# Two-layer trunk on one core: the triangular inverse on VectorE, and plain block products for the first two items of each seven-product projection

## The chip, the core and the metric

The program runs on one core of a Trainium2 chip. A core has TensorE (PE in the profile: matrix products, with its weight loads shown apart as PEld), VectorE (DVE), ScalarE (ACT), GpSimd (POOL) and SyncE (SP, which here only starts DMAs). TensorE writes to PSUM; the working memory is SBUF. The metric is the device time of one execution in microseconds: 3083.43 us is the median of three runs (3078.94 to 3089.16). The profile shows one more execution, which took 3091.84 us; its span from the first to the last instruction is 3090.0 us.

## The reference

A sequence of 1024 positions of width 1024 goes through two layers. Each layer is a mixer and a feed-forward part (FFN), both with a modulation by a condition vector and a layer norm at the end:

```
for i in range(DEPTH):
    mod = (e @ ada_w[i] + ada_b[i])[:, None, :]
    sh1, sc1, g1, sh2, sc2, g2 = jnp.split(mod, 6, axis=-1)
    y = mixers[i % N_MIXERS](x * (1.0 + sc1) + sh1)
    x = layer_norm(DN_ALPHA * x + (1.0 + g1) * y, ln_g[i, 0], ln_b[i, 0])
    y = conv_ffn(x * (1.0 + sc2) + sh2, ffn_up[i], ffn_conv_w[i], ffn_conv_b[i], ffn_down[i])
    x = layer_norm(DN_ALPHA * x + (1.0 + g2) * y, ln_g[i, 1], ln_b[i, 1])
```

The mixer of layer 0 is a gated delta net with 8 heads. It needs, for each head and each block of 64 positions, the solution of a triangular system:

```
kk = jnp.where(strict, jnp.einsum('bhncd,bhnmd->bhncm', kb, k) * decay, 0.0)
sol = lax.linalg.triangular_solve(kk + eye, rhs, left_side=True, lower=True, unit_diagonal=True)
```

and then a scan over the blocks with a state. The mixer of layer 1 is a retention with 4 heads: a projection to q, k, v and a gate of 2048 columns, a scan, and an output projection. The FFN projects 1024 to 2 x 2816 columns (gate and up), convolves the gate over three positions, and projects back.

## The kernel before

**Numbers.** Every large product is done in float32r with two halves of each operand: a value is split into a rounded high part (ScalarE copy, L89) and a low part (value minus high part, L90 on VectorE or GpSimd), and a product is three matmuls (L110 to L112). A weight block of 128 x 1024 is split whole by `load_w` (tiles wr, wh, wl); one of 128 x 512 is split by `block` (tile wb).

**Stages in order.** Gated delta net (up to about 660 us of the span), its output projection and layer norm, FFN of layer 0 (a projection up from about 775 us, a projection down), retention (its projection from about 1484 us, scan, output projection), FFN of layer 1 (projection up from about 2381 us, projection down).

**The gated delta net.** Heads go in four pairs. For a pair, `t_path` builds the blocks X, transposes them on VectorE into Y (L738), inverts the 32 x 32 triangular blocks by forward substitution (31 steps, each a product L746 into the tile fs and a subtraction L748 into T, both on GpSimd), and transposes T on VectorE into RX (L751) and a copy of it, by ScalarE, into TX (L755). `t_chain` (tile R), `prep` (L857, VectorE), `dt_half` (L892, VectorE) and `scan` use the result. `filler` gives TensorE other work meanwhile: projections of the other heads, whose convolution is three VectorE instructions per half (L450, `conv_half`), and z projections without one. The order of TensorE's instructions is written out by a planner, `run`: it keeps a clock, picks among the streams by priority, and takes the length of a wait from the table LAT; a step of the forward substitution counts LAT["fs"] = 1.03 us. On the other engines a scheduler sets the order at build time.

**The seven-product projection.** `strassen` multiplies the activations (cut in 2 x 2 blocks of four tiles each: B11, B12, B21, B22) with a list of items, each two units of 128 columns of weights. It is called three times: FFN up of layer 0, the q, k and gate projection of retention, FFN up of layer 1. An item in the steady state (`wino`, n of 2 or more) does seven block products of 12 matmuls; operand sums of the weights are formed by `psub` on VectorE in PSUM (L1131). The operand sums of the activations, T1 to T4, are formed by `build_T`: it transposes the normalized rows (L405, TensorE), scales them (L407, ScalarE), and forms T3 = B22 - B12, T2 = T3 + B11, T1 = B22 - T2 and T4 = B21 - T2, each split into halves.

B11 and B21 come from the first half of the sequence and are ready early; B12 and B22 come from the second half, whose layer norm ends just before. So the first two items are handled apart. `early` does, for each of them, the products of B11 and B21 with two blocks of the first unit (48 matmuls for both items) while the layer norm ends. Then the generators `wino(0)` and `wino(1)` form the sums of the weights on GpSimd (L1143 to L1146, tile ws), do the other five products, in two parts with the sums of `rest` between them, and add up the results on VectorE. In `build_T` the table BAL gives GpSimd the splits of T1 and T4 and one of B22 ("b1": 15, "b4": 15, "b2": 8), and the two sums of T4 are on GpSimd as well (L429, L430). GpSimd also computes a power for the layer norm (L339, L1313), which the normalization on VectorE or ScalarE (L284, L282) waits for.

Of the kernel before, what the change touches and what calls it, by code (L numbers as in the profile page):

```python
# [28 lines left out]
BAL = {"r11": 0, "r12": 0, "r22": 0, "rS1": 0, "rS2": 0, "rS3": 0, "rS4": 0, "rw21": 0, "rwT1": 0, "rwT2": 0, "rwT3": 0, "rwT4": 0, "rn": 0, "rh": 1, "011": 0, "012": 0, "022": 0, "0S1": 0, "0S2": 0, "0S3": 0, "0S4": 0, "0w21": 0, "0wT1": 0, "0wT2": 0, "0wT3": 0, "0wT4": 0, "0n": 1, "0h": 0, "f11": 0, "f12": 0, "f22": 0, "fS1": 0, "fS2": 0, "fS3": 0, "fS4": 0, "fw21": 0, "fwT1": 0, "fwT2": 0, "fwT3": 0, "fwT4": 0, "fn": 1, "fh": 0, "gw": 0, "gh": 0, "gn": 3, "b1": 15, "b2": 8, "b3": 0, "b4": 15, "bT": 0, "ba": 0, "rw11": 0, "rw22": 0, "0w11": 0, "0w22": 0, "fw11": 0, "fw22": 0}  # L29
# [4 lines left out]
def trunk_kernel(ctx: ExitStack, tc, A):  # L34
# [357 lines left out]
    def build_T(B, xts, scale, shift, tags):  # L392
        for nm in ("T1", "T2", "T3", "T4", "22"):
            B[nm] = [None] * 4
        tags = dict(zip(("T1", "T2", "T3", "T4", "22"), tags))
# [15 lines left out]
        for k, tg in enumerate((("qkv", "qkv"), ("qkv", "qkv"), ("t2", "t2"), ("t2", "ada"))):  # L411
            b12, b22 = load(k, tg[0]), load(4 + k, tg[1])
            put("22", k, b22, pool if BAL["b2"] & 1 << k else dve)
            dve.tensor_sub(b12, b22, b12)
            put("T3", k, b12, pool if BAL["b3"] & 1 << k else dve)
            raw.append((b12, b22))

        def rest():
            for k in range(4):
                t3, b22 = raw[k]  # L420
                h11, l11 = B["11"][k]
                h21, l21 = B["21"][k]
                e1 = pool if BAL["ba"] & 1 << k else dve
                e1.tensor_tensor(t3, t3, h11, ALU.add)
# [5 lines left out]
                pool.tensor_tensor(t3, t3, l21, ALU.add)  # L430
                put("T4", k, t3, pool if BAL["b4"] & 1 << k else dve)
# [1439 lines left out]
```

## Time and profile before

| | |
|---|---|
| median of three runs | 3083.43 us |
| profiled execution | 3091.84 us, span 3090.0 us |
| PE busy in the span | 2830.1 us (92%), 13434 matmuls |
| DVE busy | 2306.9 us (75%), 3705 instructions |
| ACT busy | 1316.8 us (43%) |
| POOL busy | 968.8 us (31%), 966 instructions |
| mean granted TensorE clock | 0.966 |

Busy time of PE is the sum over pipelined matmuls, so a stage with 90% can be without any gap. A timeline row gives start, length, engine, line, operation, output and input tiles, and, in brackets, the idle time in front of it with the instruction that ended it. A windows row gives, for each engine, busy time and number of instructions in a stretch, then the granted TensorE clock as a share of full speed, the DMA share and the GB/s. A waits row gives the total, the number and the longest of the waits of one kind.

### The profile page before, as it was taken

The page shows a single profiled execution, that of the slowest core. Times are in us where ns is not written, and L with a number is a line of the kernel's source. Part 1 is how long each engine was busy: PE and PEld are TensorE (multiplying, and loading weights), DVE is VectorE, ACT ScalarE, POOL GpSimd, SP SyncE. Part 2 cuts the span into 40 slices and gives each one's busy share as a digit, 9 for nine tenths or more (in the row PEclk, how much of TensorE's full clock was granted, in tenths as well). Part 3 has the DMA queues.
Part 4 walks back from the last instruction along what each step waited for, and adds up shares of the span by engine and source line. Part 5 has one row for each costly group of instructions (what it writes and reads, how often), then busy time and mean ns, then how long its engine had stood idle before and what let it go on. Part 6 is the DMA issues. An engine that isn't in the chain of part 4 may idle for free.

```text
span 3090.0 us, 38786 instructions
## 1 busy us (share of the span) xinstructions
PE 2830.1 (92%) x13434; PEld 2286.9 (74%) x13434; DVE 2306.9 (75%) x3705; ACT 1316.8 (43%) x2412; POOL 968.8 (31%) x966
## 2 busy tenths in 40 slices
PE   6979989999799999998799999999998899999996
PEld 5867767777678878786677787767776678887785
DVE  6766767465888888987777745566688987777988
ACT  3744655433444444445332342221343544444442
POOL 0366274333511111730422302522201511113604
PEclk9999999999899999999899999999999999999998
DMA  7231222243254444854233444655654242335653
GB/s 271 76 105 63 79 75 77 82 157 136 84 171 157 157 153 157 320 175 145 102 110 109 160 159 135 205 173 179 194 206 145 95 147 103 103 103 206 235 179 119
DMA packets 242596, 448.65 MB, mean 145 GB/s; under 512 B 22880, under 2 KB 76384, under 8 KB 242400
## 3 DMA queue, kind: packets, MB, share of 16 engines
q1 hardware_dynamic: 211216, 398.45, 39.0%
q10 hardware_dynamic: 29760, 43.00, 3.8%
q0 software_dynamic: 1424, 4.72, 0.4%
q8 instruction: 106, 1.74, 0.2%
q14 instruction: 90, 0.74, 0.1%
HBM read 337.55 MB, written 108.53 MB: 144 GB/s over the span
## 4 chain that ended last, share of the span: by engine, by line
PE 31%; DVE 9%; DMA 5%; issue 4%; POOL 2%; ACT 1%; SPq 0%; POOLq 0%; DVEq 0%; ACTq 0%
PE acc L580 5%; PE acc L1092 5%; PE sc L1092 2%; PE acc L110 2%; PE acc L112 2%; PE acc L111 2%; PE sc L580 2%; PE acc L275 2%; PE acc L276 2%; PE acc L277 1%; DMA wr<-in_ret_wqk 1%; PE sc L111 1%; PE sc L112 1%; PE sc L110 1%; DVE wb L90 1%
## 5 line engine op out<-in xcount | busy, mean ns | idle before, releaser
L1505 POOL TENSOR_TENSOR o<-o 128x512 f32<-128x512 f32 x88 | 117.4, 1344 | 627.2 <-DVE o L1498 618.6
L580 PE MATMUL acc<-hT,wh 128*128 128x512 f32 x960 | 300.4, 394 | 0.0
L275 PE MATMUL acc<-bb,ab 128*128 128x512 f32 x504 | 193.0, 409 | 32.6 <-DVE ab L90 18.7
L1092 PE MATMUL acc<-T,wb 128*128 128x512 f32 x840 | 207.7, 397 | 14.5 <-DVE wb L90 14.5
L276 PE MATMUL acc<-bb,ab 128*128 128x512 f32 x504 | 205.1, 407 | 9.9 <-DVE bb L90 9.8
L580 PEld LDWEIGHTS acc<-hT,wh 128*128 128x128 f32 x960 | 182.8, 190 | 33.9
L580 PE MATMUL acc<-hT,wl 128*128 128x512 f32 x480 | 203.7, 424 | 3.2 <-ACT sq L469 2.1
L90 DVE TENSOR_TENSOR ab<-ar,ab 128x512 fp32r<-128x512 f32 x210 | 181.5, 872 | 30.7 <-ACT ab L89 30.4
L89 ACT ACTIVATE ab<-ar 128x512 fp32r<-128x512 f32 x210 | 128.6, 623 | 174.8 <-PE acc L277 86.6
L277 PE MATMUL acc<-bb,ab 128*128 128x512 f32 x504 | 202.8, 404 | 0.0
L1092 PEld LDWEIGHTS acc<-T,wb 128*128 128x128 f32 x840 | 159.4, 191 | 52.7 <-DVE wb L90 19.4
L90 DVE TENSOR_TENSOR wb<-wr,wb 128x512 fp32r<-128x512 f32 x168 | 121.2, 724 | 97.8 <-ACT wb L89 96.7
L90 DVE TENSOR_TENSOR wb<-mm,wb 128x512 fp32r<-128x512 f32 x216 | 144.9, 683 | 21.0 <-ACT wb L89 19.0
L1171 ACT ACTIVATE pc<-acc 128x512 f32<-128x512 f32 x140 | 83.0, 593 | 170.1 <-PE acc L1092 99.4
L89 ACT ACTIVATE wb<-mm 128x512 fp32r<-128x512 f32 x216 | 122.5, 593 | 69.9 <-DVE mm L1131 68.1
L89 ACT ACTIVATE wb<-wr 128x512 fp32r<-128x512 f32 x168 | 102.8, 626 | 110.9 <-DMA wr<-in_ffn_up 48.0
L450 DVE SCALAR_TENSOR_TENSOR qkv<-raw,vc,qkv 128x512 f32<-128x512 f32 x144 | 125.9, 878 | 29.7 <-ACT qkv L448 26.2
L110 PE MATMUL acc<-T,wb 128*128 128x512 f32 x340 | 136.4, 403 | 11.4 <-DVE wb L90 6.4
L275 PEld LDWEIGHTS acc<-bb,ab 128*128 128x128 f32 x504 | 97.5, 195 | 61.3 <-DVE ab L90 14.3
L90 DVE TENSOR_TENSOR wl<-wr,wh 128x1024 fp32r<-128x1024 f32 x67 | 91.1, 1360 | 64.5 <-ACT wh L89 64.0
L1484 DVE SCALAR_TENSOR_TENSOR o<-g,vc,o 128x512 f32<-128x512 f32 (+2 forms) x176 | 136.5, 793 | 2.5 <-ACT o L1479 1.8
L580 PE MATMUL acc<-wh,hT 128*128 128x512 f32 x384 | 137.1, 419 | 1.2 <-DVE vv L90 1.2
(556 smaller groups left out, 8035.3 us busy)
## 6 DMA issues: line engine op xcount, KB each, us to landing
wr<-in_ffn_up SPq DMA_DIRECT2D x94, 512.0 KB, 4.1
mvw<-in_ada_w SPq DMA_DIRECT2D x80, 512.0 KB, 4.3
ad<-o SPq DMA_DIRECT2D x154, 256.0 KB, 2.1
ar<-ad SPq DMA_DIRECT2D x154, 256.0 KB, 3.8
Br<-in_ffn_down SPq DMA_DIRECT2D x88, 256.0 KB, 3.4
wr<-in_ret_wv SPq DMA_DIRECT2D x32, 512.0 KB, 3.7
ar<-od SPq DMA_DIRECT2D x56, 256.0 KB, 5.1
xs<-xt ACTq DMA_DIRECT2D x24, 512.0 KB, 4.9
```

The lines of the kernel that those rows point to most:

```text
L89: act.activation(dst_h, src, AF.Copy)
L90: eng.tensor_tensor(dst_l, src, dst_h, ALU.subtract)
L110: mm(acc, wl[:, k], hl[0], start=first, stop=False)
L111: mm(acc, wh[:, k], hl[1], start=False, stop=False)
L275: mm(acc, a[1][:, sl], w[0], start=first, stop=False)
L276: mm(acc, a[0][:, sl], w[1], start=False, stop=False)
L277: mm(acc, a[0][:, sl], w[0], start=False, stop=last)
L450: dve.scalar_tensor_tensor(oh, raw[:, 3 - j:515 - j], w[:, 3 - j:4 - j], oh, ALU.mult, ALU.add)
L580: pq(pe.matmul(out, lhsT, rhs, start=start, stop=stop), cost)
L1092: return pe.matmul(*a, skip_group_check=True, **kw)
L1484: dve.scalar_tensor_tensor(tv, gv[:, c0 - j:c1 - j], w[:, 2 - j:3 - j], tv, ALU.mult, ALU.add)
L1505: pool.tensor_tensor(o[d], o[x], o[y], op)
```

## The change

Four things change.

1. The forward substitution of the triangular inverse (L746, L748) is issued on VectorE instead of GpSimd, and LAT["fs"] goes from 1.03 to 1.3, so that the planner writes another order for TensorE in the gated delta net.
2. The first two items of each `strassen` call are computed with plain block products: eight products of 12 matmuls instead of seven, 192 matmuls for both items instead of 168. `early` is replaced by `side`. Side 0 (B11 with B21, both units of both items, 96 matmuls) comes before the transposes, side 1 (B12 with B22, 96 matmuls) after them. No sums of weights are needed, so L1143 to L1146 and the additions of the results are gone. Weights are loaded and split whole, by `load_w`, eight times per call.
3. In `build_T` B12 itself is now split and kept as well (in the buffers of T1); the sums are formed from it in another order, one more than before for each of the four tiles of T1, and all sums and all splits are on VectorE (b1, b2, b3, b4 are 0). `rest` is issued after side 1 of the first item.
4. In the retention call (`direct`) the results of side 0 go straight from PSUM through the gate's activation to memory; in the FFN calls ScalarE copies them to SBUF first.

```diff
-BAL = {... "b1": 15, "b2": 8, "b3": 0, "b4": 15, "bT": 0, "ba": 0, ...}
+BAL = {... "b1": 0, "b2": 0, "b3": 0, "b4": 0, "bT": 0, "ba": 0, ...}
...
             b12, b22 = load(k, tg[0]), load(4 + k, tg[1])
+            put("12", k, b12, pool if BAL["b3"] & 1 << k else dve)
             put("22", k, b22, pool if BAL["b2"] & 1 << k else dve)
-            dve.tensor_sub(b12, b22, b12)
-            put("T3", k, b12, pool if BAL["b3"] & 1 << k else dve)
             raw.append((b12, b22))

         def rest():
             for k in range(4):
-                t3, b22 = raw[k]
+                t1, b22 = raw[k]
                 h11, l11 = B["11"][k]
                 h21, l21 = B["21"][k]
+                dve.tensor_sub(b22, b22, t1)
+                put("T3", k, b22, pool if BAL["b3"] & 1 << k else dve)
                 e1 = pool if BAL["ba"] & 1 << k else dve
-                e1.tensor_tensor(t3, t3, h11, ALU.add)
-                e1.tensor_tensor(t3, t3, l11, ALU.add)
-                dve.tensor_sub(b22, b22, t3)
-                put("T1", k, b22, pool if BAL["b1"] & 1 << k else dve)
-                put("T2", k, t3, pool if BAL["bT"] & 1 << k else dve)
-                pool.tensor_tensor(t3, h21, t3, ALU.subtract)
-                pool.tensor_tensor(t3, t3, l21, ALU.add)
-                put("T4", k, t3, pool if BAL["b4"] & 1 << k else dve)
+                e1.tensor_tensor(b22, b22, h11, ALU.add)
+                e1.tensor_tensor(b22, b22, l11, ALU.add)
+                put("T2", k, b22, pool if BAL["bT"] & 1 << k else dve)
+                dve.tensor_sub(t1, t1, h11)
+                dve.tensor_sub(t1, t1, l11)
+                put("T1", k, t1, pool if BAL["b1"] & 1 << k else dve)
+                e4 = pool if BAL["b4"] & 1 << k else dve
+                e4.tensor_tensor(b22, h21, b22, ALU.subtract)
+                e4.tensor_tensor(b22, b22, l21, ALU.add)
+                put("T4", k, b22, e4)
...
-            pool.tensor_tensor(tv, bc(Y[:, j + 1:, j], nj), bm(T[:, j, 0:nj], ni), ALU.mult)
+            dve.tensor_tensor(tv, bc(Y[:, j + 1:, j], nj), bm(T[:, j, 0:nj], ni), ALU.mult)
             ts_ = T[:, j + 1:, 0:nj]
-            pool.tensor_tensor(ts_, ts_, tv, ALU.subtract)
+            dve.tensor_tensor(ts_, ts_, tv, ALU.subtract)
             yield LAT["fs"]
...
-        def early(u):
-            w = load_w(u)
+        def side(n, s):
             out = []
-            for b in ("11", "21"):
+            for u in items[n][:2]:
+                w = load_w(u)
                 X = acc_tile()
-                for k in range(4):
-                    mm3(X, w, k + (4 if out else 0), B[b][k], k == 0, k == 3)
-                out.append(tl("cv", [P, 516], name="p1")[:, 0:HALF])
...
+                for i, b in enumerate((("11", "21"), ("12", "22"))[s]):
+                    for k in range(4):
+                        mm3(X, w, k + 4 * i, B[b][k], i == 0 and k == 0, i == 1 and k == 3)
+                out.append(X)
             return out
...
-        ws = [wino(n, items[n][2]()) for n in range(2)]
-        for w in ws:
-            next(w)
-        rest()
...
+        for n in range(2):
+            if not direct:
+                sinks.append(items[n][2]())
+                for i in range(2):
+                    sinks[n](2 * i, ahead[n][i], None)
+            X = side(n, 1)
+            for i in range(2):
+                sinks[n](2 * i + 1, X[i], None)
+            if n == 0:
+                rest()
+            if items[n][3]:
+                items[n][3]()
+        for n in range(2, len(items)):
+            wino(n, items[n][2]())
+            if items[n][3]:
+                items[n][3]()
```

The order in which the engines get their instructions moves at three places that matter below. In the rows, the words in brackets are the semaphores that an instruction waits on, named by engine or DMA queue; line numbers of the changed kernel are 1 to 4 higher in its first half and up to 11 lower in its last part.

**VectorE at the end of the forward substitution of the first pair.** Before, VectorE runs convolutions of the filler (L450, tile qkv) and a weight split (wl), and then takes the transpose RX as soon as GpSimd has finished T:

```order
L90 TENSOR_TENSOR wl<-wr,wh 128x1024 [waits DMAHW3_49,PE_49,Activation_49]
L450 SCALAR_TENSOR_TENSOR qkv<-raw,vc,qkv 128x512 [waits DVE_49]
L450 SCALAR_TENSOR_TENSOR qkv<-raw,vc,qkv 128x512 [waits Activation_49,Pool_49]
L450 SCALAR_TENSOR_TENSOR qkv<-raw,vc,qkv 128x512 [waits DVE_49] x2
L751 STREAM_TRANSPOSE RX<-T 128x1024 [waits Pool_49]
L755 STREAM_TRANSPOSE TX<-TP 128x1024 [waits Activation_49]
L857 TENSOR_TENSOR qkv<-mm,ir 128x512 [waits PE_49]
```

In the changed kernel, at the start of the same substitution, its steps (L750 and L752) stand among the convolutions (L454):

```order
L742 STREAM_TRANSPOSE Y<-X 128x1024 [waits Activation_49]
L454 SCALAR_TENSOR_TENSOR qkv<-raw,vc,qkv 128x512 [waits DVE_49]
L750 TENSOR_TENSOR fs<-Y,T 128x31 [waits DVE_49,Pool_49]
L752 TENSOR_TENSOR T<-T,fs 128x31 [waits DVE_49]
L750 TENSOR_TENSOR fs<-Y,T 128x60 [waits DVE_49]
L454 SCALAR_TENSOR_TENSOR qkv<-raw,vc,qkv 128x512 [waits Activation_49]
L752 TENSOR_TENSOR T<-T,fs 128x30x2 [waits DVE_49]
L454 SCALAR_TENSOR_TENSOR qkv<-raw,vc,qkv 128x512 [waits DVE_49]
L750 TENSOR_TENSOR fs<-Y,T 128x87 [waits DVE_49]
```

The 62 instructions of a pair moved from GpSimd's queue into VectorE's, each behind the one before it by a wait, and other work stands between them.

**GpSimd at the layer norm in front of the retention projection.** Before, the powers for the norm (L1313, tile mv) stand behind the sums of the weights (tile ws), which wait for the DMA of the weights:

```order
L1313 TENSOR_TENSOR mv<-mv,mhalf 128x1 [waits DVE_49]
L1146 TENSOR_TENSOR ws<-wr,ws 128x512 [waits Pool_49]
L1313 TENSOR_TENSOR mv<-mv,mhalf 128x1 [waits DVE_49]
L1143 TENSOR_TENSOR ws<-wr 128x512 [waits DMAHW0_49]
L1144 TENSOR_TENSOR ws<-ws,wr 128x512 [waits DMAHW7_49,Pool_49]
L1145 TENSOR_TENSOR ws<-wr 128x512
L1313 TENSOR_TENSOR mv<-mv,mhalf 128x1 [waits DVE_49,Activation_49]
```

Now they (L1302) follow the norm's gain (L1287) directly, and the next thing on GpSimd belongs to the third item (tile rm):

```order
L1287 TENSOR_TENSOR xt<-xt,rowb 128x512 [waits DMAHW6_49,DMASW7_49]
L1287 TENSOR_TENSOR xt<-xt,rowb 128x512
L1287 TENSOR_TENSOR xt<-xt,rowb 128x512 [waits Pool_49] x3
L1302 TENSOR_TENSOR mv<-mv,mhalf 128x1 [waits DVE_49] x6
L1302 TENSOR_TENSOR mv<-mv,mhalf 128x1 [waits DVE_49,Activation_49] x2
L1529 DMA dx<-in_dx 128x1024 [waits DMAHW6_49,DMAHW4_49,PE_49]
L1561 TENSOR_TENSOR rm<-pc,sinT 128x512 [waits DMAHW2_49,DMAHW7_49,DVE_49,PE_49]
```

The sums of the weights have left the queue in front of the powers.

**The sums of the activations in the first projection.** Before, GpSimd forms T4 (L429, L430, tile bt) and splits T1, T4 and one of B22, while VectorE does the rest:

```order
L90 TENSOR_TENSOR T_7238<-bt,T_7238 128x512 [waits Activation_49]
L1146 TENSOR_TENSOR ws<-wr,ws 128x512 [waits Pool_49]
L429 TENSOR_TENSOR bt<-hT,bt 128x512 [waits DVE_49]
L90 TENSOR_TENSOR 22_7127<-bt,22_7127 128x512 [waits Activation_49]
L90 TENSOR_TENSOR T_7253<-bt,T_7253 128x512 [waits Activation_49]
L430 TENSOR_TENSOR bt<-bt,hT 128x512 [waits Pool_49]
```

In the changed kernel this is VectorE's row of work, and the two weight splits (wl) that the second half of side 1 needs on TensorE stand among it:

```order
L433 TENSOR_TENSOR bt<-hT,bt 128x512 [waits DVE_49]
L423 TENSOR_TENSOR bt<-bt 128x512 [waits DVE_49]
L434 TENSOR_TENSOR bt<-bt,hT 128x512 [waits DVE_49]
L429 TENSOR_TENSOR bt<-bt,hT 128x512 [waits DVE_49]
L430 TENSOR_TENSOR bt<-bt,hT 128x512 [waits DVE_49]
L90 TENSOR_TENSOR T_7273<-bt,T_7272 128x512 [waits Activation_49]
L90 TENSOR_TENSOR T_7278<-bt,T_7277 128x512 [waits Activation_49]
L426 TENSOR_TENSOR bt<-bt,hT 128x512 [waits DVE_49]
L90 TENSOR_TENSOR wl<-wr,wh 128x1024 [waits DMAHW4_49,PE_49,Activation_49]
L427 TENSOR_TENSOR bt<-bt,hT 128x512 [waits DVE_49]
L90 TENSOR_TENSOR wl<-wr,wh 128x1024 [waits DMAHW5_49,PE_49,Activation_49]
```

GpSimd has no part in it any more, and a weight split now has sums of `rest` ahead of it.

More of the change, by code (lines that the diff above doesn't have):

```diff
@@ L392, in build_T @@
     def build_T(B, xts, scale, shift, tags):
-        for nm in ("T1", "T2", "T3", "T4", "22"):
+        tags = dict(zip(("T1", "T2", "T3", "T4", "22"), tags))
+        tags["12"] = tags["T1"]
+        for nm in tags:
             B[nm] = [None] * 4
-        tags = dict(zip(("T1", "T2", "T3", "T4", "22"), tags))
         def put(nm, k, src, eng=dve):
@@ L1084, in c_of, with strassen @@
         return b
[L1086 removed]
+    def strassen(hT0, xts, scale, shift, items, tags=("hTb", "hTb", "qkv", "qkv", "aux"), direct=False):
         B = {"11": hT0[:4], "21": hT0[4:]}
@@ L1092, in mm_on @@
             return pe.matmul(*a, skip_group_check=True, **kw)
-        def early(u):
-            w = load_w(u)
+        def side(n, s):
             out = []
-            for b in ("11", "21"):
+            for u in items[n][:2]:
+                w = load_w(u)
                 X = acc_tile()
-                for k in range(4):
-                    mm3(X, w, k + (4 if out else 0), B[b][k], k == 0, k == 3)
-                out.append(tl("cv", [P, 516], name="p1")[:, 0:HALF])
-                if len(out) == 1:
-                    act.activation(out[0], X, AF.Copy)
-                else:
-                    dve.tensor_add(out[1], X, out[0])
-            return out
-        ahead = [early(items[n][0]) for n in range(2)]
+                for i, b in enumerate((("11", "21"), ("12", "22"))[s]):
+                    for k in range(4):
+                        mm3(X, w, k + 4 * i, B[b][k], i == 0 and k == 0, i == 1 and k == 3)
+                out.append(X)
+            return out
+        ahead, sinks = [], []
+        for n in range(2):
+            X = side(n, 0)
+            if direct:
+                sinks.append(items[n][2]())
+                for i in range(2):
+                    sinks[n](2 * i, X[i], None)
+                continue
+            ahead.append([tl("cv", [P, 516], name="ah")[:, 0:HALF] for _ in range(2)])
+            for t, x in zip(ahead[n], X):
+                act.activation(t, x, AF.Copy)
         rest = build_T(B, xts, scale, shift, tags)
@@ L1194, in strassen @@
         bg_tag[0] = "lane"
-        ws = [wino(n, items[n][2]()) for n in range(2)]
-        for w in ws:
-            next(w)
-        rest()
-        for n, it in enumerate(items):
-            for _ in ws[n] if n < 2 else wino(n, it[2]()):
-                pass
-            if it[3]:
-                it[3]()
+        for n in range(2):
+            if not direct:
+                sinks.append(items[n][2]())
+                for i in range(2):
+                    sinks[n](2 * i, ahead[n][i], None)
+            X = side(n, 1)
+            for i in range(2):
+                sinks[n](2 * i + 1, X[i], None)
[7 more added lines that the diff above has]
+                items[n][3]()
         bg_tag[0] = "wr"
@@ L1585, in sink @@
             def sink(q, a, b):
-                c = c_of(q, a, b)
-                act.activation(c, c, AF.Silu)
+                c = c_of(q, a, b) if b is not None else tl("cv", [P, 516], name="sg")[:, 0:HALF]
+                act.activation(c, a if b is None else c, AF.Silu)
                 act.dma_start(gd[u + q // 2][:, hs(q % 2)], c)
@@ L1593, in trunk_kernel @@
     B = strassen(h0, xts, sc_r, sh_r, [gate_item(0), gate_item(2)]
-                 + [rope_item(h, j) for h in range(RH) for j in range(2)] + [gate_item(u) for u in range(4, 16, 2)], ("hTa", "aux", "qkv", "qkv", "hTa"))
+                 + [rope_item(h, j) for h in range(RH) for j in range(2)] + [gate_item(u) for u in range(4, 16, 2)], ("hTa", "aux", "qkv", "qkv", "hTa"), True)
     hT = [h0, []]
```

34 lines of the change are left out of this document (2 added, 32 removed).

## The prediction

> **What bounds the kernel now.** I read the windows view first, stretch by stretch. A row gives the stretch, then busy time and number of instructions of PE, PEld, DVE, ACT and POOL, then the granted TensorE clock. The first four rows are the stretches in which GpSimd substitutes, one per pair of heads; the last three are the starts of the three projections, from the first early product to the first matmul of the third item.
>
> ```profile
> core 0: us, PE busy (x) PEld busy (x) DVE busy (x) ACT busy (x) POOL busy (x), PEclk, DMA share, GB/s
> 147.00:198.00 51.00, 40.59 (x186) 33.29 (x184) 33.58 (x36) 16.08 (x33) 45.69 (x69) 0.95 0.26 81
> 257.00:307.00 50.00, 46.61 (x264) 40.07 (x262) 30.15 (x60) 20.12 (x41) 44.55 (x74) 0.97 0.19 62
> 392.00:444.00 52.00, 48.92 (x246) 40.41 (x244) 35.81 (x49) 22.16 (x59) 47.71 (x72) 1.00 0.28 87
> 515.00:568.00 53.00, 46.96 (x258) 39.18 (x257) 36.36 (x63) 25.44 (x64) 48.72 (x74) 1.00 0.23 75
> 775.00:844.00 69.00, 53.23 (x206) 40.65 (x205) 61.10 (x75) 35.64 (x57) 44.05 (x31) 0.83 0.24 83
> 1484.00:1558.00 74.00, 55.61 (x203) 41.74 (x202) 57.11 (x72) 33.12 (x56) 38.61 (x30) 0.82 0.32 110
> 2381.00:2446.00 65.00, 49.83 (x201) 37.79 (x201) 57.68 (x68) 29.97 (x50) 43.29 (x31) 0.89 0.29 98
> ```
>
> Everywhere else TensorE sets the pace; in the last three stretches it does not. There VectorE is busy 57 to 61 us with only 68 to 75 instructions, GpSimd 39 to 44 us, and the TensorE clock falls to 0.82 to 0.89. The timeline says why (start, length, engine, line):
>
> ```profile
> 799.23 1.75 DVE L424 TENSOR_TENSOR bt<-bt,hT 128x512 f32<-128x512 f32 x1
> 810.46 1.71 POOL L430 TENSOR_TENSOR bt<-bt,hT 128x512 f32<-128x512 f32 x1
> 812.64 0.68 DVE L424 TENSOR_TENSOR bt<-bt,hT 128x512 f32<-128x512 f32 x1
> 813.24 0.68 DVE L90 TENSOR_TENSOR T<-bt,T 128x512 fp32r<-128x512 f32 x1
> 783.53 1.29 POOL L1143 TENSOR_TENSOR ws<-wr 128x512 f32<-128x512 f32 x1 [1.54 <-DMA wr<-in_ffn_up]
> ```
>
> The same sum of two SBUF tiles takes VectorE 1.75 us while GpSimd sums beside it and 0.68 us when GpSimd stands still (812.64); GpSimd takes 1.71 us beside VectorE and 1.29 us alone. Each slows the other, so a share of such sums on GpSimd gains nothing here: both together do two in 1.75 us, VectorE alone does two in 1.28 (812.64 to 813.24 for the first, 0.68 for the second). What TensorE makes of it:
>
> ```profile
> 775.64 0.39 PE L110 MATMUL acc<-hT,wl 128*128 128x512 f32 x1
> 786.29 0.40 PE L112 MATMUL acc<-hT,wh 128*128 128x512 f32 x1
> 804.39 0.80 PE L111 MATMUL acc<-22_7105,wb 128*128 128x512 f32 x1 [4.47 <-DVE 22_7105 L90]
> 811.09 0.80 PE L111 MATMUL sc<-T,wb 128*128 128x512 f32 x1 [4.63 <-DVE T L90]
> 814.58 0.80 PE L110 MATMUL acc<-22_7061,wb 128*128 128x512 f32 x1 [0.98 <-DVE wb L90]
> 820.72 0.41 PE L112 MATMUL acc<-T,wb 128*128 128x512 f32 x1
> 843.67 0.40 PE L110 MATMUL acc<-hT,wb 128*128 128x512 f32 x1
> ```
>
> 48 early matmuls go from 775.64 to 786.29 (0.227 us each), then come waits for VectorE, and from 814.58 to 820.72 fourteen matmuls take 6.14 us, 0.44 each, at half the pace. Item three begins at 843.67: 68.0 us for 168 matmuls that need 38.1. The other two calls begin and end here, the second with its norm:
>
> ```profile
> 1483.92 0.39 PE L110 MATMUL acc<-hT,wl 128*128 128x512 f32 x1
> 1490.28 0.14 DVE L1312 TENSOR_SCALAR mv<-mv 128x1 f32<-128x1 f32 x1
> 1497.02 0.55 POOL L1313 TENSOR_TENSOR mv<-mv,mhalf 128x1 f32<-128x1 f32 x1
> 1497.61 1.74 DVE L284 TENSOR_SCALAR xt<-xt,mv 128x1024 f32<-128x1024 f32 x1 [4.27 <-POOL mv L1313]
> 1499.40 0.44 PE L405 MATMUL mm<-cst,xt 128*128 128x128 f32 x2 [3.99 <-DVE xt L284]
> 1508.64 1.04 PE L405 MATMUL mm<-cst,xt 128*128 128x128 f32 x8
> 1557.58 0.39 PE L110 MATMUL acc<-hT,wb 128*128 128x512 f32 x1
> 2381.06 0.39 PE L110 MATMUL acc<-hT,wl 128*128 128x512 f32 x1
> 2397.94 0.69 PE L405 MATMUL mm<-cst,xt 128*128 128x128 f32 x2 [5.13 <-DVE xt L284]
> 2445.23 0.39 PE L110 MATMUL acc<-hT,wb 128*128 128x512 f32 x1
> ```
>
> 73.7 and 64.2 us; together 205.9. VectorE had the variance at 1490.28, and GpSimd raised it to its power only at 1497.02, behind the sums of the weights: TensorE stands 3.99 us, and 5.13 in the third call.
>
> **The starts of the projections, part by part.** *TensorE:* 192 matmuls x 0.227 = 43.6 us, 5.4 more than now; 32 transposes at 1.04 for eight, 4.2; together 47.8. One more weight block of 512 KB is loaded per call (8 for 7); with a DMA share of 0.24 to 0.32 in these stretches I cost that at nothing, and if the load came late its landing would be the price. *The norm:* GpSimd's queue has no sums in it any more, so the power follows the variance, and 96 early matmuls (21.8 us) stand where 48 did; the waits of 3.99 and 5.13 go. *VectorE:* in the changed order 24 instructions stand between the arrival of the second tile of B12 and the two weight splits (wl) without which side 1 of the second item can't start: 24 x 0.60, and 0.6 more for each wl, which is twice as long: 15.6 us. Behind these two splits only the second unit's matmuls and the rest of `rest` are queued. TensorE has the last 24 transposes and the first item's 48 matmuls to do meanwhile, 3.1 + 10.9 = 14 us; the first transposed tile reaches VectorE through ScalarE a microsecond or two later, so TensorE waits about 3 (4 in the first call, where the same count gives one instruction pair more). Behind such a wait I expect fourteen matmuls at half pace again: 14 x (0.44 - 0.227) = 3.0 us. So 54.8, 53.6 and 53.6 us, 162.0 in all, 43.9 less than 205.9. When the third item starts VectorE still has the end of `rest` and the first item's convolution to do; I price what that delays at 2 us a call, 6. Net **-38**. Bounds: with no wait and no half pace 3 x 47.8 = 143.4, -62; with 1.2 us an instruction (half of them beside something else), 24 x 0.6 = 14 us more a call, about 0.
>
> The Trainium skill ("TensorE: Matmul & The Clock Gate", Part 1, "What's actually happening") has the slow state last until one window of about 3.4 us has been busy. The rows above show 6.14 us of it. By the page the half pace would cost 1.6 instead of 3.0 us a call, an estimate, and the sum would be 4 us lower. Here the trace decides.
>
> **The substitution.** What it costs now, and what VectorE's prices are:
>
> ```profile
> L748 POOL TENSOR_TENSOR T<-T,fs 128x31 f32<-128x31 f32 (+15 forms) x124 | 86.9, 700 | 8.5
> L746 POOL TENSOR_TENSOR fs<-Y,T 128x31 f32<-128x31 f32 (+15 forms) x124 | 82.5, 666 | 19.1 <-DVE Y L738 10.9
> 20.97 5.48 DVE L504 SCALAR_TENSOR_TENSOR mva<-mvw,e,mva 128x512 f32<-128x512 f32 x7
> L936 DVE TENSOR_TENSOR qkv<-qkv,acc 128x128 f32<-128x128 f32 x56 | 15.6, 278 | 2.5 <-PE acc L580 2.3
> 146.30 1.25 DVE L738 STREAM_TRANSPOSE Y<-X 128x1024 f32<-128x1024 f32 x1 [0.40 <-ACT X L734]
> 197.88 1.25 DVE L751 STREAM_TRANSPOSE RX<-T 128x1024 f32<-128x1024 f32 x1 [7.55 <-POOL T L748]
> 201.75 2.08 PE L580 MATMUL mm<-qkv 128*128 128x128 f32 x8 [13.03 <-DVE qkv L857]
> 273.99 0.49 PE L580 MATMUL sc<-Sn,qkv 128*128 128x128 f32 x2 [2.42 <-DVE Sn L928]
> ```
>
> On GpSimd 169 us, 42 a pair. No row shows these shapes on VectorE. 0.278 us for 128 elements and 0.68 for 512 give 0.144 + 1.047 ns an element; a chain in which each needs the one before (L504: 0.783 each) adds some 0.04. A pair has 31 steps, 62 instructions and 2 x 5456 elements (11.4 us): 62 x 0.184 + 11.4 = 22.8 us. Ends: at the pace of independent ones, 0.60 for 512, an instruction costs 0.064 beside its elements, 62 x 0.064 + 11.4 = 15.4 us; at GpSimd's price 42. I take 22.8, the same engine's chained price.
>
> VectorE gets 91 us more, but it is in order, and the changed order has 38, 62, 83 and 59 other instructions inside the four substitutions (34, 59, 48 and 62 before). At the same prices these are 26.5, 25.1, 36.9 and 22.7 us; with 22.8 each, 49, 48, 60 and 46 us from Y to RX. Before it was 50.3 (146.30 + 1.25 to 197.88) and 50 to 53 for the others. So T comes hardly earlier. What changes is TensorE's order: with 1.3 us a step the planner puts 93 more filler matmuls ahead of the first pair's use of T, 21 us, which cover the 13.03 us for which TensorE stands at 201.75. These are TensorE's waits from 145 to 660 us:
>
> ```profile
> PE mm L580 <- DVE qkv L857: 19.7, 3, 13.0
> PE acc L583 <- ACT qkv L451: 13.4, 2, 11.8
> ```
>
> The 19.7 belong to three pairs whose use of T now stands behind 93, 63 and 24 more fillers, counted in the order; I let them go. The 11.8 belong to the third pair, with a longer window and fewer fillers; I keep them. On the other side, the fillers spent early are missing in the first pair's scan, where five double steps now follow each other without any, two before: 3 x 2.42 (the wait at 273.99) = 7.3. And 55 links of the scan (u and Sn) now share VectorE with substitution steps, half a step of 0.37 us at about every second one: 5 us. Net **-7** (-19.7 + 7.3 + 5). Bounds: -33 (all of these waits go), and +70 with GpSimd's price on VectorE: 42 - 22.8 = 19.2 us longer in each of four windows, 77, and TensorE full in them, so that nothing hides it.
>
> The Trainium skill, in "VectorE: DVE Perf Modes" ("The DRAIN you can't avoid"), says that a semaphore between two instructions costs nothing. The rows disagree: 0.783 us chained against 0.60 to 0.68. By the page a pair would cost the lower end given above, which is the larger gain below.
>
> Sum: -38 - 7 = -45, from 3091.84 (span 3090.0 and 1.8 around it) to 3047 for a profiled execution; the median lies 8.4 lower, so **3038 us**.
>
> **The rivals.** *Smaller gain, 3063.* The sums and splits of `build_T` on VectorE, each low part behind ScalarE's high part of the same tile, don't run back to back but at 0.9 us: 24 x 0.3 = 7.2 us more a call, 22 in all, -38 becomes -16, and the delta net gives half of its 7: -20. For it: one in-order queue that alternates with another. Against: before, with GpSimd still, such a pair ran 0.60 apart (812.64, 813.24).
>
> *Larger gain, 2993.* VectorE is quicker than I price it. At the independent pace, 15.4 us a pair, Y to RX is 7 us shorter, T is there before it is asked for, and the 33 us go; without the waits for wl and their half pace the starts gain 62 less the 6 behind them, 56. Together -90. For it: these 33 us are all that stands between TensorE and a full stage. Against: 60 us of listed work in the third pair's window.
>
> *Slower, 3115.* The substitution runs on VectorE at GpSimd's price: strided and broadcast operands of shapes that no row shows. -45 + 77 = +32. It decides once a step (now 22.8 / 31 = 0.74 us) takes 45 / (4 x 31) = 0.36 more, 1.1 us. For it: VectorE would have no gap in these windows, so weight splits and convolutions for TensorE's fillers are late too. Against: the same engine has shown 0.278 us for 128 elements.
>
> That the change doesn't do what it says the order excludes: the 248 instructions and all sums stand in VectorE's queue.
>
> **How the numbers follow.** Forecast 0.55, smaller gain 0.22, larger 0.10, slower 0.09, gains and losses that cancel 0.04. About 0.3% (9 us) is what a measurement can tell from no change. The forecast's own range is 3018 to 3058. The whole range, 3000 to 3072, takes in the smaller gain with some room and most of the way to the larger; outside lie slower, nothing and the far parts of these two, 0.2. Faster: 0.55 + 0.10 + 0.20 of the smaller gain = 0.85; same 0.04 + 0.02 = 0.06; slower 0.09.
>
> **What would show it.** Right: VectorE's sums at 0.68 us throughout the three starts; from first early product to third item 51 to 57 us each; no wait of L406 on the norm; one wait of 2 to 6 us on wl ahead of side 1 of the second item; substitution instructions of 0.17 to 0.42 us; Y to RX 45 to 62 us; no 13 us wait near 200 us. Wrong: VectorE's sums above 0.9 us with GpSimd idle, starts over 62 us, or waits of TensorE on L454 and L90 inside the substitution windows that add up to more than the 33 us that stood there.

## The result, and the profile after

The changed kernel takes 3035.52 us (median of four runs, 3032.59 to 3043.01) against 3083.55 for the kernel before; the ratio is 0.9847, with a 95% interval of 0.9821 to 0.9873. The forecast was 3038 us. A second set of five runs gave 0.9838 (0.9826 to 0.9850). The profiled execution has a span of 3036.6 us, 53.4 less than the 3090.0 of before. The stretches in which it went, each from the first matmul of one stage to the first of the next:

| us | before | predicted change | after | change |
|---|---|---|---|---|
| up to the first early product of the first projection | 775.6 | -7 | 760.9 | -14.7 |
| the three starts of a projection, together | 205.9 | -43.9 | 168.1 | -37.8 |
| all the rest | 2108.5 | +6 | 2107.6 | -0.9 |

The windows view of the changed kernel, same stages and columns as in the prediction (the four substitutions, then the three starts):

```profile
core 0: us, PE busy (x) PEld busy (x) DVE busy (x) ACT busy (x) POOL busy (x), PEclk, DMA share, GB/s
149.00:200.00 51.00, 51.00 (x230) 42.25 (x230) 45.72 (x102) 21.83 (x48) 2.62 (x5) 1.00 0.30 98
268.00:318.00 50.00, 48.71 (x278) 41.62 (x277) 46.09 (x126) 26.91 (x82) 6.73 (x12) 1.00 0.19 63
379.00:440.00 61.00, 59.14 (x322) 50.02 (x323) 57.84 (x147) 32.35 (x82) 9.06 (x14) 1.00 0.27 87
508.00:556.00 48.00, 44.15 (x242) 38.49 (x242) 45.12 (x123) 22.91 (x46) 8.03 (x13) 0.93 0.13 49
761.00:816.50 55.50, 50.45 (x226) 39.86 (x224) 42.44 (x74) 32.59 (x48) 2.84 (x4) 0.97 0.34 122
1460.00:1517.00 57.00, 52.07 (x226) 41.33 (x225) 41.69 (x66) 26.98 (x43) 2.26 (x4) 0.94 0.36 130
2338.50:2394.50 56.00, 50.84 (x228) 40.48 (x227) 43.33 (x69) 27.02 (x43) 1.99 (x3) 0.97 0.29 104
```

In the starts VectorE runs nearly as many instructions as before (66 to 74) in 42 to 43 us instead of 57 to 61, and the TensorE clock is 0.94 to 0.97 instead of 0.82 to 0.89. In the substitutions VectorE takes over 62 instructions in each and is busy 45 to 58 of 48 to 61 us.

The timeline of the first start, VectorE's sums, then the one large wait, and the first matmul of the third item:

```profile
796.29 0.70 DVE L90 TENSOR_TENSOR 22_7184<-bt,22_7184 128x512 fp32r<-128x512 f32 x1
796.89 0.70 DVE L430 TENSOR_TENSOR bt<-bt,hT 128x512 f32<-128x512 f32 x1
...
800.86 0.60 ACT L1457 ACTIVATE g<-acc 128x512 f32<-128x512 f32 x1 [0.28 <-PE acc L112]
800.89 0.39 PE L112 MATMUL acc<-22_7184,wh 128*128 128x512 f32 x1
801.36 1.05 ACT L89 ACTIVATE wh<-wr 128x1024 fp32r<-128x1024 f32 x1
802.57 1.22 DVE L90 TENSOR_TENSOR wl<-wr,wh 128x1024 fp32r<-128x1024 f32 x1
803.84 0.50 PE L110 MATMUL acc<-12_7121,wl 128*128 128x512 f32 x1 [2.56 <-DVE wl L90]
805.13 0.53 PE L112 MATMUL acc<-12_7141,wh 128*128 128x512 f32 x1
808.44 0.49 PE L111 MATMUL acc<-22_7124,wh 128*128 128x512 f32 x1
...
816.50 0.39 PE L110 MATMUL sc<-hT,wb 128*128 128x512 f32 x1
```

VectorE's sums are 0.70 us long and 0.60 apart. TensorE waits 2.56 us for wl, and from 805.13 to 808.44 eight matmuls take 3.31 us, 0.41 each (3.3 and 3.4 us at half pace in the other two starts). The starts last 55.6, 56.9 and 55.6 us.

The substitution, by groups of the whole program and at the end of the first pair:

```profile
L752 DVE TENSOR_TENSOR T<-T,fs 128x31 f32<-128x31 f32 (+15 forms) x124 | 42.2, 341 | 1.8
L750 DVE TENSOR_TENSOR fs<-Y,T 128x31 f32<-128x31 f32 (+15 forms) x124 | 42.0, 339 | 1.5
147.90 1.25 DVE L742 STREAM_TRANSPOSE Y<-X 128x1024 f32<-128x1024 f32 x1 [0.41 <-ACT X L738]
199.50 0.19 DVE L752 TENSOR_TENSOR T<-T,fs 128x31 f32<-128x31 f32 x1
199.73 1.25 DVE L755 STREAM_TRANSPOSE RX<-T 128x1024 f32<-128x1024 f32 x1
213.95 0.38 PE L584 MATMUL mm<-qkv 128*128 128x128 f32 x1 [3.51 <-DVE qkv L861]
```

84.2 us on VectorE, 21.1 a pair, where GpSimd took 169. From Y to RX the first pair takes 50.6 us (147.90 + 1.25 to 199.73), the others 49.2, 59.7 and 46.0. The wait of 13.03 us near 200 is now 3.51.

### The profile page after: what moved, and what is told of

It reads as the page before. It is cut to its first block, busy times and chain, and to the rows that moved or that the text cites. A ratio compares the mean times of both kernels' runs of the same rounds, so it can differ in the third digit from the quotient of the medians.

```text
span 3036.6 us, 38865 instructions
## 1 busy us (share of the span) xinstructions
PE 2830.3 (93%) x13506; PEld 2295.6 (76%) x13506; DVE 2314.2 (76%) x3974; ACT 1307.9 (43%) x2398; POOL 683.3 (23%) x637
## 4 chain that ended last, share of the span: by engine, by line
PE 57%; DVE 22%; DMA 9%; issue 6%; ACT 5%; POOL 2%; SPq 0%; DVEq 0%; POOLq 0%; ACTq 0%
PE acc L584 11%; PE acc L1096 7%; PE acc L110 4%; PE acc L111 4%; PE acc L112 4%; PE sc L1096 4%; PE sc L584 3%; PE acc L275 3%; PE acc L277 3%; PE acc L276 3%; DMA mvw<-in_ada_w 2%; PE mm L584 2%; DVE qkv L454 2%; DVE wb L90 2%; PE sc L110 1%
## 5 line engine op out<-in xcount | busy, mean ns | idle before, releaser
L1096 PE MATMUL acc<-T,wb 128*128 128x512 f32 x840 | 205.1, 393 | 9.4 <-DVE wb L90 9.4
L90 DVE TENSOR_TENSOR wb<-wr,wb 128x512 fp32r<-128x512 f32 x162 | 114.7, 710 | 91.8 <-ACT wb L89 90.1
L90 DVE TENSOR_TENSOR wl<-wr,wh 128x1024 fp32r<-128x1024 f32 x85 | 108.6, 1278 | 97.4 <-ACT wh L89 97.2
L89 ACT ACTIVATE wh<-wr 128x1024 fp32r<-128x1024 f32 x101 | 106.8, 1059 | 107.9 <-PE acc L584 56.0
L213 DVE SCALAR_TENSOR_TENSOR ada<-mvw,e,ada 128x512 f32<-128x512 f32 x140 | 108.1, 772 | 27.9 <-DMA mvw<-in_ada_w 27.2
```

The lines of the kernel that those rows point to most:

```text
L89: act.activation(dst_h, src, AF.Copy)
L90: eng.tensor_tensor(dst_l, src, dst_h, ALU.subtract)
L1096: return pe.matmul(*a, skip_group_check=True, **kw)
```

## The experiments

Two questions: does the gain before the first projection come from TensorE's new order, as the prediction has it, or from the engine that does the work; and what holds the starts.

**e1: the substitution alone, in the new order.**

```diff
-            pool.tensor_tensor(tv, ...)
+            dve.tensor_tensor(tv, ...)
...
-            pool.tensor_tensor(ts_, ts_, tv, ALU.subtract)
+            dve.tensor_tensor(ts_, ts_, tv, ALU.subtract)
...
-    LAT = {... "fs": 1.03, ...}
+    LAT = {... "fs": 1.3, ...}
```

> The kernel before with the first of the four changes alone: forward substitution on VectorE and 1.3 us a step in the planner's table; the starts of the projections are as before. Theory (the parts add up): the first projection starts near 761 us of the span instead of 775.6, the three starts stay at 68, 74 and 64 us, the time is about 3069 us (-15). Rival (the gain up to the first projection comes from the norm and the weights of the starts, not from the substitution): first projection near 770 to 775, time 3078 to 3084.

Measured: ratio 0.9959 (0.9944 to 0.9975), 13 us. The first projection starts at 755.3 us; the starts are 71.5, 73.2 and 63.5. It is a gain of its own, of the expected size.

**e2: the substitution alone, in the old order.** As above, with 1.03 left.

> Substitution on VectorE, but with the old 1.03 us a step in the planner's table, so TensorE's order is that of the kernel before. Theory (the gain comes from the changed order of TensorE, which puts fillers in front of the first use of T): the 13.0 us wait near 200 us of the span stays (10 to 14 us), the first projection starts at 772 to 780, the time is 3080 to 3088. Rival (the gain comes from the engine, by freeing GpSimd and by short links): the first projection starts near 763, the time is about 3071.

Measured: 0.9949 (0.9934 to 0.9964), 15 us, and the first projection at 754.0 us. The rival holds: the engine makes the gain, in either order. At the place of the 13.03 us most of the wait is left, while the 11.80 us of the third pair, which the prediction kept, are gone (a wait of 6.16 us for DT at 444.9 us stands there instead). The rows are of this kernel and of the kernel before, with VectorE's own wait for GpSimd over the four substitutions of the latter:

```profile
204.71 0.58 PE L580 MATMUL mm<-qkv 128*128 128x128 f32 x1 [8.31 <-DVE DT L892]
```

```profile
455.10 0.48 PE L583 MATMUL acc<-cst,qkv 128*128 128x128 f32 x1 [11.80 <-ACT qkv L451]
L751 DVE STREAM_TRANSPOSE RX<-T 128x1024 f32<-128x1024 f32 x4 | 5.0, 1245 | 15.5 <-POOL T L748 15.5
```

Before, VectorE stood 15.5 us in front of the four transposes RX, for a T that GpSimd had not finished, and the convolutions behind in its queue stood with it. Matched one by one up to the first projection, TensorE's matmuls (the order is the same but for 60 of some 4200) run ahead of the kernel before by 1.1 us at the second pair's Y, by 7 at the third pair's, 13 at the fourth pair's, and 21 to 22 from 595 us on: the gain comes after the first substitution. Two more waits fall, both between 147 and 605 us: VectorE's waits for ScalarE in front of the convolutions go from 20.5 to 4.9 us, and those for GpSimd's job `so` (L954), which mostly stood behind steps of the substitution in GpSimd's queue, from 6.8 us to none.

**e3: the order alone.** Only 1.03 to 1.3; the substitution stays on GpSimd.

> Only the planner's number goes to 1.3 us a step; the substitution stays on GpSimd. Theory (the order makes the gain): the 13.0 us wait near 200 us falls under 4, the first projection starts at 762 to 768, the time is 3070 to 3076. Rival (the engine makes it): the first projection starts at 773 to 779, the time is 3081 to 3087.

Measured: 1.0077 (1.0057 to 1.0096), 24 us slower, with the first projection at 791.6 us. Neither theory had this. The order that puts more fillers ahead of the first use of T costs 16 us there as long as GpSimd does the work; TensorE's waits up to the first projection add up to 102.2 us, 98.1 before. The other 12 us are longer busy time of TensorE (688.9 us for 677.0), at a granted clock of 0.93 to 0.95 from 145 us on, where it was 0.95 to 0.97. Why the fillers are missed so much more with GpSimd was not traced further.

**e4: the starts alone.** The changed kernel with the substitution on GpSimd and 1.03.

> The changed kernel with the substitution back on GpSimd and 1.03 us a step: only the starts of the three projections are changed. Theory (the parts add up): first projection near 773 to 776 us, the three starts 55 to 57 us each, the time is about 3046 us (-38). Rival (the starts gain only because the stages before leave VectorE and GpSimd less behind): first start over 60 us, time over 3055.

Measured: 0.9902 (0.9886 to 0.9919), 30 us where 38 were expected; starts 54.0, 55.3 and 56.8. The starts gain on their own what they gain in the whole; the rest of the difference is the stretch behind the first of them, 7 us longer than before (647.3 for 640.2). The two halves multiply to 0.9959 x 0.9902 = 0.9861, and the whole is 0.9847 and 0.9838: they add up within their intervals.

**e5: GpSimd's shares put back into the changed starts.**

```diff
-BAL = {... "b1": 0, "b2": 0, "b3": 0, "b4": 0, ...}
+BAL = {... "b1": 15, "b2": 8, "b3": 0, "b4": 15, ...}
```

> The changed kernel with the shares of GpSimd in the sums of the activations put back (the splits of T1 and T4 and one of B22, and the two sums of T4); plain products for the first two items stay. Theory (what the starts lost was lost to sums that run on both engines at once): VectorE's sums take 1.7 us again where GpSimd works, the three starts grow from 56 to 60 to 65 us, the time is 3050 to 3062. Rival (96 matmuls in front of the transposes and 96 behind cover the sums on any engine): starts 55 to 58 us, time 3033 to 3040.

Measured: 0.9884 (0.9865 to 0.9903), which is 11 to 14 us more than the changed kernel's 0.9847 and 0.9838. The starts are 59.2, 57.8 and 59.1, less growth than expected; the wait for wl is 5.32, 4.10 and 3.85 us, and the stretches behind the first two starts are 5 and 7 us longer. Sums on both engines cost time even with 96 matmuls in front and behind. How one engine stops the other, in the timeline of this kernel:

```profile
789.73 0.68 DVE L429 TENSOR_TENSOR bt<-bt,hT 128x512 f32<-128x512 f32 x1
789.89 2.88 POOL L90 TENSOR_TENSOR T<-bt,T 128x512 fp32r<-128x512 f32 x1 [24.89 <-DVE 12_7181 L90]
790.34 0.68 DVE L90 TENSOR_TENSOR T<-bt,T 128x512 fp32r<-128x512 f32 x1
790.94 0.68 DVE L430 TENSOR_TENSOR bt<-bt,hT 128x512 f32<-128x512 f32 x1
792.73 1.29 POOL L90 TENSOR_TENSOR 22_7184<-bt,22_7184 128x512 fp32r<-128x512 f32 x1
793.98 1.29 POOL L433 TENSOR_TENSOR bt<-hT,bt 128x512 f32<-128x512 f32 x1
794.05 1.76 DVE L423 TENSOR_TENSOR bt<-bt 128x512 f32<-128x512 f32 x1 [2.43 <-POOL 22_7184 L90]
795.34 1.60 POOL L434 TENSOR_TENSOR bt<-bt,hT 128x512 f32<-128x512 f32 x1
```

L423 starts 0.07 us after GpSimd's L433 and ends 0.54 us after it, where a sum alone is 0.68 us long: it stood still for nearly all of GpSimd's instruction, and then ran. The other way round, GpSimd's first split starts 0.16 us after VectorE's L429 and takes 2.88 us; it ends 1.15 us after the last of VectorE's three sums (791.62), and 1.29 is its length alone.

**e6: seven products kept, all sums on VectorE.** The kernel before with b1, b2 and b4 at 0 and the two sums of T4 on VectorE; the weight sums stay on GpSimd.

> The kernel before with one part of the change: all sums and splits of the activations on VectorE, while the first two items keep their seven products and their weight sums on GpSimd. Theory (the two engines slow each other): the starts fall from 68, 74 and 65 us to about 62, 66 and 60, the time by some 15 us. Rival (the seven products need their operands early, so VectorE alone is the bound, and only the plain products cure it): starts 68 to 76 us, time within 6 us of the kernel before or above it.

Measured: 0.9938 (0.9923 to 0.9953), 19 us; starts 61.6, 59.8 and 58.8, together 180.2. So of the 38 us in the starts 26 come from taking the sums off GpSimd (205.9 to 180.2), and 12 from the plain products and what goes with them (180.2 to 168.1). The waits for the norm (3.57 and 4.61 us here) are still there, and belong to these 12: the power still queues behind the weight sums.

**e7: buffers of their own for the second item's weights.** In the changed kernel the two weight blocks of side 1 of the second item go to tiles that nothing else uses there, and their splits stand ahead of `rest`.

```diff
-            X = side(n, 1)
+            X = side(n, 1, pre if n else None)
...
             if n == 0:
+                pre = [load_q(u) for u in items[1][:2]]
                 rest()
```

> The changed kernel, but the two weight blocks of side 1 of the second item are split into buffers of their own, in program order ahead of the sums of rest (half blocks of 128 x 512, so four splits more per call). Theory (the wait for wl of 2.4 to 2.7 us is the release of the first item's weight buffers, then the ScalarE and VectorE splits one after the other): that wait is gone in all three calls and so is the half pace behind it, starts 51 to 53 us, time 3024 to 3028. Rival (VectorE is the bound there, by the 24 instructions that the prediction counted): TensorE waits as long at the tiles of B12, B22 or at the first operand of the third item, starts 55 to 57, time 3033 to 3040.

Measured: 0.9798 (0.9775 to 0.9822), the best of all kernels; the change itself had 0.9838 (0.9826 to 0.9850) in its larger set, and the two were not timed side by side. The wait for wl is gone in all three starts, most of the waits on B12's tiles are gone with it, and the starts are 51.0, 49.6 and 49.0: VectorE's list of sums is not what held them. The experiment also moves the splits ahead of `rest`, so that by itself it does not tell the two theories apart; the changed kernel's timeline does. There VectorE's split of wl starts 0.16 us after ScalarE's split of wh ends (802.41), so the list of sums costs that much at most, and 2.3 of the 2.56 us are the two splits, one after the other, behind the first item's last matmul. Whether ScalarE stood there for the buffers or for its own queue, in which the instruction in front (L1457 at 800.86) waits for the first item as well, is not told apart. The starts are 18.5 us shorter together (149.6 for 168.1); 10.4 come back behind the first of them (654.2 us for 643.8), where TensorE now waits in the third item:

```profile
820.81 0.80 PE L1097 MATMUL acc<-T,wb 128*128 128x512 f32 x1 [4.69 <-ACT T L89]
```

**e8: work for nothing on GpSimd during the substitutions.** In the changed kernel, 93 added sums of 128 x 128 in each window, of constants, which nobody waits for:

```diff
+            for _ in range(3):
+                pool.tensor_tensor(scr, flat(Y)[:, 0:P] if j == _ == 0 else cst[:, 0:P], cst[:, P:2 * P], ALU.add)
             yield LAT["fs"]
```

> The changed kernel with work for nothing on GpSimd: in each of the four substitution windows 93 sums of 128 x 128 of two SBUF tiles (some 41 us at the old price of such instructions), which nobody waits for; the first one waits for Y. Theory (half of the gain before the first projection is that VectorE no longer shares with GpSimd): the convolution instructions of VectorE in these windows go from 0.755 back to 0.85 to 0.90 us on average, the first projection starts at 766 to 774 instead of 761, the time is 3041 to 3050. Rival (the gain is that VectorE's queue no longer stops for GpSimd's T): the convolutions are slower, but the first projection starts within 3 us of 761, time 3033 to 3039.

Measured: ratio 1.0000 (0.9989 to 1.0010): all of the gain is gone. The starts keep theirs (55.6, 55.3 and 56.9); the first projection starts at 807.2 us, 46 later than in the changed kernel (50 later than in its second profile, e9), and Y to RX takes 66.4, 59.2, 75.6 and 55.0 us. That is far beyond the theory's 5 to 13 us, in its direction. VectorE's groups from 147 us to behind the fourth window (570 us, and 605 in this kernel), of the kernel before, of the changed kernel and of this one, and last GpSimd's added sums:

```profile
L450 DVE SCALAR_TENSOR_TENSOR qkv<-raw,vc,qkv 128x512 f32<-128x512 f32 x106 | 94.9, 896 | 20.3 <-ACT qkv L448 17.0 <-POOL raw L442 1.4 <-POOL raw L444 1.1
L955 DVE TENSOR_TENSOR qkv<-qkv,so 128x512 f32<-128x512 f32 x12 | 11.8, 980 | 6.8 <-POOL so L954 6.8
L866 DVE TENSOR_TENSOR U<-mm,eg 128x512 f32<-128x512 f32 x12 | 8.2, 686 | 6.0 <-PE mm L583 6.0
```

```profile
L454 DVE SCALAR_TENSOR_TENSOR qkv<-raw,vc,qkv 128x512 f32<-128x512 f32 x110 | 83.1, 755 | 10.1 <-ACT qkv L452 9.6
L959 DVE TENSOR_TENSOR qkv<-qkv,so 128x512 f32<-128x512 f32 x12 | 8.2, 687 | 0.4 <-POOL so L958 0.4
L870 DVE TENSOR_TENSOR U<-mm,eg 128x512 f32<-128x512 f32 x12 | 8.2, 685 | 3.0 <-PE mm L587 3.0
```

```profile
L455 DVE SCALAR_TENSOR_TENSOR qkv<-raw,vc,qkv 128x512 f32<-128x512 f32 x106 | 91.6, 864 | 2.9 <-ACT qkv L453 2.8
L962 DVE TENSOR_TENSOR qkv<-qkv,so 128x512 f32<-128x512 f32 x12 | 10.6, 880 | 3.3 <-POOL so L961 3.1
L751 DVE TENSOR_TENSOR fs<-Y,T 128x31 f32<-128x31 f32 (+15 forms) x124 | 61.0, 492 | 1.6
L753 DVE TENSOR_TENSOR T<-T,fs 128x31 f32<-128x31 f32 (+15 forms) x124 | 60.5, 488 | 1.8
L873 DVE TENSOR_TENSOR U<-mm,eg 128x512 f32<-128x512 f32 x12 | 8.2, 684 | 2.1 <-PE mm L588 2.1
L755 POOL TENSOR_TENSOR scr<-cst 128x128 f32<-128x128 f32 x354 | 213.6, 603 | 24.9
```

The same instruction is slower with GpSimd at work, 0.896 and 0.864 against 0.755 us for the convolution, 0.49 against 0.34 for a substitution step's half (37 us in all). L866, L870 and L873, one of whose operands (mm) is in PSUM, stay at 0.684 to 0.686 us in all three. This kernel loses more than the kernel before since here the substitution, too, is on the slowed engine. The added sums also stand in front of GpSimd's own small jobs, but that is a small part: VectorE and ScalarE wait 7.5 us for GpSimd in this stretch, 4.6 in the changed kernel.

**e9: the change again, beside three variants.**

> The changed kernel itself, beside the next three on one chip. Its profile of the first time had the first projection at 760.9 us, while three kernels with the same work up to that point had 755 to 756. Theory (that was the spread of one execution): first projection at 754 to 761, starts 55 to 57 us each, ratio to the kernel before 0.982 to 0.987. Rival (the early products of the changed starts delay what stands in front of them): first projection at 760 to 762 again.

Measured: 0.9838 (0.9826 to 0.9850); first projection at 756.8 us, starts 55.3, 55.4 and 55.6. The 760.9 of the first profile was the spread of one execution.

**e10: T1 first.** The own buffers of e7, and `rest` in two passes: T1 of all four tiles, then T3, T2 and T4.

```diff
             for k in range(4):
                 dve.tensor_sub(b22, b22, t1)
-                put("T3", k, b22, ...); ...; put("T2", k, b22, ...)
                 dve.tensor_sub(t1, t1, h11)
                 dve.tensor_sub(t1, t1, l11)
                 put("T1", k, t1)
+            for k in range(4):
+                put("T3", k, b22)
+                ...
+                put("T2", k, b22)
                 ...
                 put("T4", k, b22)
```

> Own buffers for the weights of side 1 of the second item as in e7, and in rest the four tiles of T1 are formed ahead of those of T3, T2 and T4. Theory (the 4.6 us that TensorE waits for T inside the third item of e7 are T1's splits, behind eight other sums and splits, in buffers that B12 still holds): this wait falls under 1.5 us, starts 52 to 54 us, time 8 to 14 us below the changed kernel of the same call. Rival (VectorE has a fixed amount to do before the third item runs freely, whatever the order): the wait moves to T2 or the weights of the third item, time within 5 us of the changed kernel.

Measured: 0.9835 (0.9822 to 0.9848), equal to the change, as the rival had it. The starts are those of e7, 51.0, 49.7 and 49.0, 17 us less than the change beside it; the two stretches with an FFN behind them take 12 and 11 us more (656.4 for 644.0 and 652.6 for 641.8), the retention's 8 less, about what it differs by between the change's own two profiles (821.5 and 828.2). The wait in the third item is still there:

```profile
829.97 0.79 PE L1098 MATMUL acc<-T,wb 128*128 128x512 f32 x1 [5.29 <-ACT T L89]
```

L1098, like L1097 above, is the line of products that are added onto an accumulator, T2's first. In e7 TensorE waited for the last tile of T2, and T1's came half a microsecond behind it; here T1 is done by 816.6, and forming it first moved T2 further back. My reading of the wait in e7 was wrong.

**e11: the change in the old order.** Only 1.3 back to 1.03.

> The changed kernel with 1.03 us a step in the planner's table, so TensorE has the order of the kernel before up to the first projection; the substitution is on VectorE. By the first pair of runs (substitution alone, in both orders) the order is worth nothing: first projection at 752 to 758 us, time within 5 us of the changed kernel of the same call. By the prediction's account (the fillers ahead of the first use of T pay): first projection at 767 or later, time 7 to 15 us above it.

Measured: 0.9856 (0.9842 to 0.9870), 4.8 us above the change beside it, with intervals that overlap; first projection at 755.9 us. The order is worth 5 us at most, and nothing of it shows ahead of the first projection.

**e12: T1 first, weight buffers shared.**

> The changed kernel with T1 formed first in rest, its weights in the shared buffers as they are. Theory (two separate waits: the weight buffers ahead of the second item's side 1, and T1 in the third item): the wait of 2.4 to 2.7 us for wl stays, the waits in the first 40 us behind the start of the third item fall from 11.3 us in all three calls to under 7, time 2 to 6 us below the changed kernel. Rival (T1 earlier only delays the weight split behind it): the wait for wl grows to 3.5 to 5 us, time equal or above.

Measured: 0.9909 (0.9895 to 0.9922), 22 us slower than the change beside it: the rival's direction, without its cause. The wait for wl stays (2.44, 2.44 and 1.99 us) and the starts are 55.4, 55.2 and 53.3, but the stretches with an FFN behind them take 15 and 12 us more (659.5 for 644.0, 653.8 for 641.8), with waits of 8.4 and 9.1 us in their first 60 us where the change has 5.5 and 4.1. The order T3, T2, T1, T4 in `rest` serves the third item better.

## Why the prediction was right, and where its steps were not

*What bounds the starts.* Right. Two-operand sums on both engines were the cause: VectorE's sums are at 0.70 us, taking the sums off GpSimd alone brings 26 of the 38 us (e6), and putting GpSimd's shares back costs 11 to 14 us (e5).

*The sum for the starts, -43.9, and +6 behind them.* Measured -37.8, and behind the starts 3.9 us more of TensorE's waits (in the 40 us behind each: 2.9, 0.5 and 4.0 us before, 5.8, 2.2 and 3.3 after), which the rest of the program made up for. The net, -38, stands against -38.7 for starts and rest. Inside the sum three things differ. The wait for wl was sized well (3 to 4; measured 2.56, 2.44 and 2.69), but the step "24 instructions stand between the arrival of the second tile of B12 and the two weight splits" failed as a cause: the blocks of the second item share two buffers with those of the first, so that ScalarE's split (801.36) starts only when the first item's last matmuls have run (800.89), for the buffers or for the queue in front of it, and VectorE's follows (802.57). With buffers of their own, and the splits ahead of the sums, the wait was gone. The half pace was mis-sized: eight matmuls at 0.41 us, not fourteen at 0.44, so 1.5 us a call and not 3.0. The Trainium skill's window of 3.4 us ("TensorE: Matmul & The Clock Gate", Part 1, "What's actually happening") was the better guide here: 3.31 us after, though 6.14 before. And waits on the tiles of B12, some 2.2 us a call in pieces of 0.2 to 1.5, were left out.

*The substitution's price.* Right: 21.1 us a pair for 22.8 predicted, and 50.6, 49.2, 59.7 and 46.0 us from Y to RX for 49, 48, 60 and 46. The slower rival, GpSimd's price on VectorE, falls with it.

*What the substitution is worth, -7.* This step failed: "What changes is TensorE's order". The order, alone, costs 24 us; the engine, in the old order, brings 15 in the whole time and 22 ahead of the first projection. (The 14.7 us of the table are at the low end: the kernels e1, e2, e5, e7 and e9 to e12, all with the substitution on VectorE, start the first projection at 754.0 to 759.9 us, 16 to 22 earlier than before.) T does come no earlier, as predicted; but VectorE no longer stops at RX for GpSimd (15.5 us), its convolutions and weight splits no longer share with it (a convolution's instruction goes from 0.896 to 0.755 us, 15 us over some 106 of them, a split of wl between 147 and 605 us from 1.44 to 1.22), and GpSimd's own small jobs no longer stand behind the steps (6.8 us of waits for `so`). All three reach TensorE through the fillers, and so the 11.80 us that the prediction kept are gone. The prediction had used uncontended prices for the changed kernel, but had not asked what contended ones cost the kernel before inside the substitutions, as it had done for the starts. How much of this is the queues and how much the sharing stays open. The idle load of e8 shows that sharing alone can cost more than all of it, but it does not size the sharing of before: 37 us of what VectorE's instructions lose there are the substitution's own steps, which were not on VectorE then; the convolutions lose 12.

*The rivals.* The smaller gain (0.9 us a sum) and the larger (all waits gone) did not come; the two errors, -7 for -15 and -44 for -38, partly made up for each other. The profiled executions differ by 53 us and the medians by 48, where 45 were forecast: that the median came within 3 us is in part luck.

## What to carry to other kernels

Price a pair of engines, not an engine: before giving GpSimd a share of two-operand SBUF work, or keeping one there, look in the trace for the same VectorE instruction beside it and without it. A move off GpSimd can pay although the result is ready no earlier, since the queue of the receiving engine no longer stops for it, and its instructions no longer stand still beside it; here both changed together. And a wait that ends on a split is not always a wait for the splitting engine: look for what held the split itself (here the end of the first item, through a shared buffer or a queue), before shortening the engine's list.

## What was not expected of the hardware

The slowdown between VectorE and GpSimd is a standstill, not a sharing of pace, in the rows of e5, and it depends on where the operands lie. There a VectorE sum of 0.68 us took 1.76, its end 0.54 us behind that of GpSimd's sum; instructions of VectorE with one operand in PSUM kept 0.684 to 0.686 us beside a busy GpSimd. The Trainium skill, "SBUF — State Buffer" ("Who interferes with whom"), has this rule: a VectorE instruction with two SBUF inputs contends with a GpSimd instruction that reads SBUF, the one that comes second blocks for the whole instruction, and one with at most one SBUF input, outside the two-port modes, isn't touched. The rows of e5 and e8 shown above agree with it, in both orders. Its size was the surprise: some 214 us of GpSimd sums which nobody needed cost 46 to 50 us before the first projection, as much as the whole change gains.
